# Two halves of a head weighed in a row, y split at its gating, and a second place for transposed weights

## The chip, the core and the metric

The kernel runs on one core of one Trainium2 chip. A core has five engines that run their own instruction streams: TensorE (PE, matrix products; its weight loads are shown as PEld), VectorE (DVE), ScalarE (ACT), GpSimd (POOL) and SyncE (SP), which here only issues transfers. TensorE writes into PSUM, eight banks of 128 partitions; the other data stand in SBUF. The metric is the time of one execution on the device in microseconds; lower is better.

## The reference

The program is two decoder layers over 1024 positions of width 1024, and a last RMS norm. Layer 0 is a gated linear recurrence (RG-LRU), layer 1 is attention with a forget gate (FoX). The change touches layer 1:

```python
u = h @ w_in                      # q, k, v, gate: 16 heads of 64
cum = jnp.cumsum(jax.nn.log_sigmoid(f_logit), axis=1)
logits = q @ k.T * scale + (cum_q - cum_k)
p = jax.nn.softmax(jnp.where(causal, logits, NEG_INF))
o = p @ v                         # "weighing"
y = o * jax.nn.silu(gate)         # "gating"
x = x + y @ w_out
```

## The kernel before

**Numbers in two parts.** Layer 1 keeps float32 accuracy with float16 products: every operand is a high part (the value rounded to float16) and a low part (what is left). A product of two such operands is three matmuls: high by high, low by high, high by low. In the weighing, two of the three share one matmul: V's high and low columns of a head (64 + 64) stand side by side as one 128-wide stationary operand against the high weights ("high", 128 wide), and the low weights go against V's high columns alone ("low", 64 wide). These low matmuls alternate between the left and the right 64 columns of the array, so that two run at a time, and land in the upper or lower half of the same PSUM bank `O`. The two halves of the bank are added when it is read (ScalarE copies one, VectorE adds the other; `yo`).

**Tiling of a head.** Rows (queries) are cut into two halves of 512, `c` = 0 and 1, and these into four blocks of 128. `maxima(hd, c)` does four steps, one for each block `i`: the logits `S` (TensorE, against 128 to 1024 keys), mask and minimum (VectorE, L1086), the exponential (ScalarE), normalised high part `pp` (ScalarE) and low part (VectorE, L1099), and a transposing DMA on SP's queue into `pT` (L1101). `weigh(hd, c)` (L1107) multiplies the transposed weights with V: 4 key blocks for half 0, 8 for half 1, some cut short by causality (512, 384, 256, 128 columns; for half 1 five of 512, then 384, 256, 128). `gated` (L1137) multiplies a pair of heads with its gate `sg`, after the pair's odd head.

**What is woven in.** TensorE is kept busy by other work between these steps: `fill` (the projections for the next pair's q, k and gate, `play`; from head 12 on the partial output projections `partial`, then the last ones in `turned`), and `vals` (V of the next group of four heads, `values_beside`, 16 steps over four heads, a step is 12 matmuls of 256 columns). A fill step is six matmuls of 512 columns.

**What sets the order.** `run` (L1155) plays a string: a digit takes the next step of that generator (0 the weighing, 1 the row blocks), "." a fill step and a piece of a load for T and U (`side`), "v" a value step, "w" a step of the value weights. Each step's TensorE instructions are tied behind the TensorE instruction that was written last (`tc.issue_after`), so the string is TensorE's order. A head has two phases: first `weigh(hd, 0)` beside `maxima(hd, 1)`, then `weigh(hd, 1)` beside `maxima(hd + 1, 0)`. The strings ORDER, TURN, OPEN, START and LAST (L29 to L33) serve plain heads, heads 3 and 7, heads 4 and 8, head 0, and heads 12 to 14; head 15 has its own. What is not tied is placed by a planner, which takes instructions in program order as they become ready and free slots allow, and puts in the semaphores. Each engine then runs its stream in order.

**Places.** A pool tag is a number of slots; a new tile waits until the last reader of the slot's old tile is done. `pT0` and `pT1` (transposed weights of half 0 and 1) have one slot each, `O`, `S` and `g` in PSUM two each. `hT` has two tags of 16 slots of 2 KB: `hh` holds the input of layer 1 (`h16`), `hl` holds 12 gated results `y` in float32 (`kept_y`, pairs 0 to 5), and later x for the first half (`xh`) and results (`res`).

**y.** For pairs 0 to 5 the gated y is kept in float32 (L1145) and split into high and low in heads 12 and 13, beside the last gate projection (`split_loaded`, `beside`): one ScalarE and one VectorE instruction on 128 x 512 for each of 12. Pairs 6 and 7 are split when they are gated (`split_y`).

**Output weights.** `split_out` (L1200) loads `wo` on SP's queue into the three `wf` slots and splits it. `partial` (L1224) fetches x on GpSimd's queue into its `home` and adds the product over pairs 0 to 5.

Of the kernel before, what the change touches and what calls it, by code (L numbers as in the profile page):

```python
# [43 lines left out]
def trunk(ctx: ExitStack, tc: tile.TileContext, xt, w0, wg, wo0, pc, gn, gf, w1, wv, wf, bf, wo1, out):  # L44
# [163 lines left out]
    with nullcontext(ExitStack()) as l0:  # L208
# [8 lines left out]
        def pair():  # L217
            return tuple(hpool.tile([P, HALF], F32R, tag=t, name=t) for t in ("hh", "hl"))
# [48 lines left out]
        raw = [[pair() for k in range(KT)] for h in range(2)]  # L267
# [446 lines left out]
    with ExitStack() as l1:  # L714
# [172 lines left out]
        kept_y = [[hpool.tile([P, HALF], F32, tag="hl", name="y") for pair in range(6)] for c in range(2)]  # L887
# [176 lines left out]
        def maxima(hd, c):  # L1064
# [6 lines left out]
            turned_ = pT[c] = at.tile([P, 4 * c + 4, 2, HALF], FP16, tag=f"pT{c}", name="pT", bufs=1)  # L1071
# [35 lines left out]
        def weigh(hd, c, sub=slice(0, HALF)):  # L1107

            pair, s = hd // 2, hd % 2
            V, turned_ = Vs[pair], pT[c]  # L1110
# [8 lines left out]
            def weighed(to, v, j, t, **kw):  # L1119
                q = max(begin, j * P)  # L1120
                matmul(to[:, q - begin :], v, turned_[:, j, t, q - c * HALF : end - c * HALF], **kw)

            for j in range(nj):
                weighed(O, V[j][:, 2 * s : 2 * s + 2].rearrange("p a d -> p (a d)"), j, 0, start=j == 0, stop=False)
                if j % 2 and j < nj - 1:
                    yield
            for j in range(nj):
                side = (j ^ (j >> 1) if j >= nj - 4 else j) % 2
                weighed(O[side * HD :][:HD], V[j][:, 3 * s], j, 1, start=False, stop=j >= nj - 2)

            r0, r1 = s * HD, (1 - s) * HD
            to, one = yo[r0 : r0 + HD], unit_v[:, hd // 4 : hd // 4 + 1]
            nc.scalar.activation(to, O[r1 : r1 + HD], AF.Copy, scale=one[r1 : r1 + HD])
            nc.vector.scalar_tensor_tensor(to, O[r0 : r0 + HD], one[r0 : r0 + HD], to, ALU.mult, ALU.add)
            yield

        def gated(hd, c, sub=slice(0, HALF)):  # L1137

            if hd % 2 == 0:
                return  # L1140
            pair = hd // 2
            yo = to = yos[pair, c][:, sub]
            if pair < 6:
                to = kept_y[c][pair][:, sub]
            nc.vector.tensor_tensor(  # L1145
                to, yo, sgs[pair][:, c * HALF + sub.start : c * HALF + sub.stop], ALU.mult
            )
            if hd == 15:
                split_y(c, pair, yo, sub)
# [31 lines left out]
        def high_y(c):  # L1181
            for pair in range(6):
                pair_of_y(c, pair)
            yield from ()

        def split_loaded(c):
            for pair in range(6):
                y = kept_y[c][pair]
                split_16(y, *y1[c][pair])
                if pair % 2:  # L1190
                    yield

        def beside(steps, first, more):

            for i, _ in enumerate(steps):
                if i >= first:
                    next(more, None)
                yield
# [70 lines left out]
        def turned(c, q):  # L1269
# [4 lines left out]
            if c == 0:  # L1274
                res = [[hpool.tile([P, HALF], F32, tag="hl", name="res") for h in range(2)] for b in range(2)]
# [100 lines left out]
        for hd in range(HEADS):  # L1376
            pair = hd // 2
            if hd % 2 == 0:
                if hd < 12:
                    fill = play(next(fills))  # L1380
                elif hd == 12:
                    todo = [(db, c) for c in range(2) for db in range(2)]
                    todo += [(db, c) for db in range(2, KT) for c in range(2)]
                    splits = [split_loaded(c) for c in range(2)]
# [20 lines left out]
            run(first, weigh(hd, 0), maxima(hd, 1), fill=fill, side=side, vals=vals, wvals=wvals)  # L1405
# [6 lines left out]
            gated(hd, 0)  # L1412
# [5 lines left out]
            run(second, weigh(hd, 1), maxima(hd + 1, 0), fill=fill, side=side, vals=vals, wvals=wvals)  # L1418
# [3 lines left out]
            drain(side)  # L1422
            gated(hd, 1)
# [7 lines left out]
        run("0..0..0...0..", weigh(15, 1, quarters[0]), fill=fill)  # L1431
        gated(15, 1, quarters[0])
        run("0..0..0..0...0..", weigh(15, 1, quarters[1]), fill=fill)
# [76 lines left out]
```

## Time and profile before

| what | value |
| --- | --- |
| three timed runs | 1020.7, 1019.57, 1020.6 us (median 1020.6) |
| the profiled execution | 1016.93 us |
| its span, first to last instruction | 1015.2 us |
| PE, DVE, ACT, POOL busy | 98%, 78%, 66%, 11% of the span |
| granted TensorE clock | 0.999 |

The profile is of one execution, whose own time differs from the median of the timed runs by 3.7 us. The weighings of the 16 heads start between 527.2 and 994.7 us; layer 0 lies before them, the end of the output projection and the last norm behind. A matmul's shown length includes its way through the array: the next starts before it has ended, so that the distance from start to start is what it costs.

### The profile page before, as it was taken

What the parts mean: (1) busy time and instruction counts of PE and PEld (TensorE: products, weight loads), DVE (VectorE), ACT (ScalarE), POOL (GpSimd) and SP (SyncE); (2) the same over time, 40 slices, a digit from 0 to 9 for tenths busy, and PEclk for the clock granted to TensorE, in tenths of its full rate; (3) what the DMA queues carried; (4) which work ended last, traced back from release to release, by engine and by line L of the source; (5) the groups of instructions that cost most, each with busy time, mean ns of one, the idle gap of its engine ahead of it and who ended that gap; (6) DMA issues with size and microseconds to landing.
All of it is one profiled execution on the core that took longest, in us unless ns stands there. A gap on an engine that the chain in (4) does not pass through costs nothing. (4 is left out here: it accounts for less than half of the span.)

```text
span 1015.2 us, 15117 instructions
## 1 busy us (share of the span) xinstructions
PE 995.4 (98%) x5100; PEld 655.3 (65%) x5100; DVE 788.4 (78%) x1500; ACT 669.1 (66%) x1219; POOL 110.4 (11%) x104
## 2 busy tenths in 40 slices
PE   9999999999999999999999999999999999999997
PEld 6787778888888888776545555555555555444454
DVE  7689585586567557898687988988898878995875
ACT  8469855657657567576684667776667666873655
POOL 1310221222122122000200000000010000001200
PEclk9999999999999999999999999999999999999999
DMA  7211443243334333244366687977688677777954
GB/s 256 62 51 48 126 140 97 91 133 103 124 106 131 96 107 113 70 148 137 85 157 124 122 151 147 193 152 150 130 202 136 138 160 150 154 180 185 231 101 167
DMA packets 219629, 135.88 MB, mean 134 GB/s; under 512 B 162080, under 2 KB 186464, under 8 KB 219552
## 3 DMA queue, kind: packets, MB, share of 16 engines
q1 hardware_dynamic: 216912, 126.27, 51.5%
q0 software_dynamic: 2640, 8.65, 3.1%
q8 instruction: 40, 0.66, 0.3%
q14 instruction: 37, 0.30, 0.1%
HBM read 75.16 MB, written 9.37 MB: 83 GB/s over the span
## 5 line engine op out<-in xcount | busy, mean ns | idle before, releaser
L72 PE MATMUL gps<-h,w 128*128 128x512 f16 x1152 | 268.0, 379 | 0.0
L72 PEld LDWEIGHTS <-w 128*128 128x128 f16 x1440 | 139.9, 98 | 156.3 <-issue 6.8
L60 ACT ACTIVATE p<-p,m 128x128 f32<-128x128 f32 (+7 forms) x128 | 98.9, 772 | 84.1 <-DVE m L1086 75.4
L114 POOL TENSOR_TENSOR wl<-wf,wh 128x512 fp32r<-128x512 f32 x46 | 82.0, 1791 | 315.9 <-ACT wh L60 258.5
L1086 DVE CUSTOM_DVE_ANT_0 p<-S,mask,vsq 128x128 f32<-128x128 f32 (+7 forms) x128 | 103.6, 810 | 14.6 <-PE S L72 14.2
L1099 DVE SCALAR_TENSOR_TENSOR pp<-p,sums,pp 128x128 f16<-128x128 f32 (+7 forms) x128 | 103.4, 812 | 12.2 <-ACT pp L60 11.7
L60 ACT ACTIVATE pp<-p,sums 128x128 f16<-128x128 f32 (+7 forms) x128 | 97.9, 768 | 20.1 <-ACT p L60 14.4
L60 ACT ACTIVATE wsf<-wsf 128x512 f32<-128x512 f32 (+1 forms) x81 | 50.5, 625 | 60.5 <-DMA wsf<-in_w 33.0
L72 PEld LDWEIGHTS <-h 128*128 128x128 f16 x768 | 74.8, 98 | 21.0 <-ACT h L60 1.3
L72 PE MATMUL S<-T,U 128*128 128x512 f16 (+4 forms) x384 | 83.4, 327 | 0.1
L72 PE MATMUL ops<-yh,wh 128*128 128x512 f32 x192 | 77.2, 402 | 1.6 <-ACT yh L60 0.9
L72 PE MATMUL ups<-hh,wh 128*128 128x512 f32 x192 | 76.3, 398 | 1.0 <-ACT hh L60 0.8
L72 PE MATMUL ups<-hl,wh 128*128 128x512 f32 x192 | 76.2, 397 | 0.2 <-DVE hl L275 0.2
L72 PE MATMUL ops<-yh,wl 128*128 128x512 f32 x192 | 75.7, 394 | 0.8 <-DVE wl L114 0.8
L72 PE MATMUL ups<-hh,wl 128*128 128x512 f32 x192 | 75.6, 394 | 0.8 <-POOL wl L114 0.8
L72 PE MATMUL gps<-hh,wh 128*128 128x512 f32 x192 | 75.8, 395 | 0.0
L72 PE MATMUL gps<-hh,wl 128*128 128x512 f32 x192 | 75.5, 393 | 0.1
L72 PE MATMUL gps<-hl,wh 128*128 128x512 f32 x192 | 75.4, 393 | 0.0
L72 PE MATMUL ops<-yl,wh 128*128 128x512 f32 x192 | 74.5, 394 | 0.0
L413 DVE TENSOR_TENSOR x<-x,ops 128x512 f32<-128x512 f32 x80 | 53.7, 679 | 24.8 <-PE ops L72 24.4
L72 PE MATMUL ops<-y,w 128*128 128x512 f16 x288 | 67.5, 379 | 3.5 <-DVE sg L1055 2.2
L72 PE MATMUL vps<-wv,h 128*128 128x256 f16 x576 | 70.4, 273 | 0.0
(253 smaller groups left out, 1764.8 us busy)
## 6 DMA issues: line engine op xcount, KB each, us to landing
wf<-in_w SPq DMA_DIRECT2D x106, 256.0 KB
wsf<-in_w SPq DMA_DIRECT2D x48, 256.0 KB
wf<-in_wo SPq DMA_DIRECT2D x64, 128.0 KB
x<-in_xt SPq DMA_DIRECT2D x16, 256.0 KB
wsf<-in_wv SPq DMA_DIRECT2D x16, 256.0 KB
wsf<-in_wo SPq DMA_DIRECT2D x16, 256.0 KB
x1d<-x SPq DMA_DIRECT2D x16, 256.0 KB
T<-qkh SPq DMA_DIRECT2D x64, 64.0 KB
```

What stands on the lines that cost most here:

```text
L60: act[0] = op(*args, **kw)
L72: pe[0] = nc.tensor.matmul(*args, **kw)
L114: return eng.tensor_tensor(lo, src, f32(hi), ALU.subtract)
L413: nc.vector.tensor_tensor(x, x, pt, ALU.add)
L1086: nc.vector.tensor_tensor_reduce(p, S[:, :n], mask[:, SEQ - n :], unit_s[:, pair : pair + 1], -NEG, ALU.add, ALU.min, accum_out=m)
L1099: nc.vector.scalar_tensor_tensor(both[:, :, 1], p, r, both[:, :, 0], ALU.mult, ALU.subtract)
```

## The change

Four things are edited.

- **Weighing.** Phase one of a head has no weighing any more (the strings lose their "0", a fill step takes its place). Phase two weighs both halves at its end: high of half 0, low of half 0, low of half 1, high of half 1 (`weigh_both`, six steps). Head 15 keeps one half at a time (`weigh_one`). Since the order within half 1 is turned round, each side of the bank notes whether it has been started. TURN loses one "v".
- **A second place for half 0's transposed weights.** Odd heads put them into a new tag `hx` in `hT`, even ones into `pT0` as before. `hx` takes the room of four slots of `hl`, which shrinks from 16 to 12; in layer 0 it holds four low parts of x.
- **y.** For pairs 0 to 5 gating now multiplies with the gate and the scale of y in one VectorE instruction, a ScalarE copy makes the high part and a GpSimd subtraction the low part, into float16 tiles in `hl`. Gating of both halves comes after phase two. `high_y`, `split_loaded` and `beside` go, and what they did beside head 12's and 13's work.
- **Output projection.** The weights for the first two column blocks are loaded on GpSimd's queue at head 12, into the slots that the value weights had (`load_out`). x for the first half and its results go to `hh`.

```diff
-ORDER = "1.v1..1.v1..00", "1.v1..1.v1..0000"
-TURN = "w1v.v1w.w.1w..1w..0000"
-OPEN = "1..1..1..1vv.00", "1..1..1v.1v.0000"
-START = "w1..1.w1..1.00", "1v.1.v.1v.1v.0000"
-LAST = "1..1..1..1..0.0", "1..1.1..1..0..0.0.0"
+ORDER = "1.v1..1.v1...", "1.v1.1.v1..000000"
+TURN = "w1v.1w.w.1w..1w..000000"
+OPEN = "1..1..1..1vv..", "1..1v.1v.1..000000"
+START = "w1..1.w1..1..", "1v.1.v.1v.1v.000000"
+LAST = "1..1..1..1...", "1..1.1..1..0..00.0.00"
...
-            return tuple(hpool.tile([P, HALF], F32R, tag=t, name=t) for t in ("hh", "hl"))
+            return tuple(hpool.tile([P, HALF], F32R, tag=t, name=t, bufs=b) for t, b in (("hh", 16), ("hl", 12)))
...
-        raw = [[pair() for k in range(KT)] for h in range(2)]
+        raw = [[pair() for k in range(KT - 4 * h)] for h in range(2)]
+        low = hpool.tile([P, 4, HALF], F32R, tag="hx", name="hx", bufs=1)
+        raw[1] += [(hpool.tile([P, HALF], F32R, tag="hh", name="hh"), low[:, k]) for k in range(4)]
...
-        kept_y = [[hpool.tile([P, HALF], F32, tag="hl", name="y") for pair in range(6)] for c in range(2)]
+        for c, pair in itertools.product(range(2), range(6)):
+            y = hpool.tile([P, 2, HALF], FP16, tag="hl", name="y16", bufs=12)
+            y1[c][pair] = y[:, 0], y[:, 1]
...
-            turned_ = pT[c] = at.tile([P, 4 * c + 4, 2, HALF], FP16, tag=f"pT{c}", name="pT", bufs=1)
+            if s and c == 0:
+                turned_ = hpool.tile([P, 4, 2, HALF], FP16, tag="hx", name="pT", bufs=1)
+            else:
+                turned_ = at.tile([P, 4 * c + 4, 2, HALF], FP16, tag=f"pT{c}", name="pT", bufs=1)
+            pT[hd, c] = turned_
...
+            begun = [False, False]
+
+            def weighed(to, v, j, t, sides, **kw):
                 q = max(begin, j * P)
+                new = not all(begun[i] for i in sides)
+                for i in sides:
+                    begun[i] = True
+                matmul(to[:, q - begin :], v, turned_[:, j, t, q - c * HALF : end - c * HALF], start=new, **kw)
+
+            def high(last):
+                for j in range(nj):
+                    v = V[j][:, 2 * s : 2 * s + 2].rearrange("p a d -> p (a d)")
+                    weighed(O, v, j, 0, (0, 1), stop=last and j == nj - 1)
+                    if j % 2 and j < nj - 1:
+                        yield
+
+            def low(last):
+                for j in range(nj):
+                    side = (j ^ (j >> 1) if j >= nj - 4 else j) % 2
+                    weighed(O[side * HD :][:HD], V[j][:, 3 * s], j, 1, (side,), stop=last and j >= nj - 2)
...
+        def weigh_one(*args):
+            high, low, out = weigh(*args)
+            yield from high(False)
+            low(True)
+            out()
+            yield
+
+        def weigh_both(hd):
+            high, low, out = weigh(hd, 0)
+            yield from high(False)
+            low(True)
+            out()
+            high, low, out = weigh(hd, 1)
+            low(False)
+            yield
+            yield from high(True)
+            out()
             yield
...
-            yo = to = yos[pair, c][:, sub]
+            yo = yos[pair, c][:, sub]
+            g_ = sgs[pair][:, c * HALF + sub.start : c * HALF + sub.stop]
             if pair < 6:
-                to = kept_y[c][pair][:, sub]
...
+                yh, yl = y1[c][pair]
+                nc.vector.scalar_tensor_tensor(yo, yo, scale_y, g_, ALU.mult, ALU.mult)
+                with tc.issue_after(seen[0].ins):
+                    to_hi(yh, yo, nc.scalar)
+                nc.gpsimd.tensor_tensor(yl, yo, yh, ALU.subtract)
+            else:
+                nc.vector.tensor_tensor(yo, yo, g_, ALU.mult)
...
+        def load_out(db):
+            for k, n in ((0, 4), (4, 2)):
+                raw_o[db, k] = at.tile([P, n, P], F32, tag="wv", name="wof", bufs=4)
+                nc.gpsimd.dma_start(raw_o[db, k], wo1[db, :, k : k + n])
...
-                    wo[db] += cast16(*load16([(wo1[db, :, k : k + n], slice(0, P))], (n, P), None), scale_o)
+                    wt = raw_o[db, k] if db < 2 else load16([(wo1[db, :, k : k + n], slice(0, P))], (n, P), None)[0]
+                    wo[db] += cast16(wt, None, scale_o)
...
-                x = hpool.tile([P, HALF], F32, tag="hl", name="xh")
+                x = hpool.tile([P, HALF], F32, tag="hh", name="xh")
...
-                res = [[hpool.tile([P, HALF], F32, tag="hl", name="res") for h in range(2)] for b in range(2)]
+                res = [[hpool.tile([P, HALF], F32, tag="hh", name="res") for h in range(2)] for b in range(2)]
...
-                        high_y(0),
                         first_out(),
-                        beside(play(last_g[1]), 1, splits[0]),
-                        high_y(1),
-                        beside(partial(todo), 3, splits[1]),
+                        play(last_g[1]),
+                        partial(todo),
...
-            run(first, weigh(hd, 0), maxima(hd, 1), fill=fill, side=side, vals=vals, wvals=wvals)
+            weighing = weigh_one(15, 0) if hd == HEADS - 1 else iter(())
+            run(first, weighing, maxima(hd, 1), fill=fill, side=side, vals=vals, wvals=wvals)
...
-            gated(hd, 0)
...
-            run(second, weigh(hd, 1), maxima(hd + 1, 0), fill=fill, side=side, vals=vals, wvals=wvals)
+            run(second, weigh_both(hd), maxima(hd + 1, 0), fill=fill, side=side, vals=vals, wvals=wvals)
...
+            gated(hd, 0)
             gated(hd, 1)
```

More of the change, by code (lines that the diff above doesn't have):

```diff
@@ L1127, in weigh @@
[L1127 to L1134, printed above, removed]
+                new = not all(begun[i] for i in sides)
@@ new lines, in out @@
+            def out():
+                r0, r1 = s * HD, (1 - s) * HD
+                to, one = yo[r0 : r0 + HD], unit_v[:, hd // 4 : hd // 4 + 1]
+                nc.scalar.activation(to, O[r1 : r1 + HD], AF.Copy, scale=one[r1 : r1 + HD])
+                nc.vector.scalar_tensor_tensor(to, O[r0 : r0 + HD], one[r0 : r0 + HD], to, ALU.mult, ALU.add)
+            return high, low, out
+        def weigh_one(*args):
[4 more added lines that the diff above has]
+            yield
@@ L1179, in split_y @@
             split_16(y, yh, yl)
[L1181 to L1198, printed above, removed]
+        raw_o = {}
+        def load_out(db):
+            for k, n in ((0, 4), (4, 2)):
+                raw_o[db, k] = at.tile([P, n, P], F32, tag="wv", name="wof", bufs=4)
+                nc.gpsimd.dma_start(raw_o[db, k], wo1[db, :, k : k + n])
         def split_out(db):
@@ L1430, in trunk @@
         gated(15, 0)
-        run("0..0..0...0..", weigh(15, 1, quarters[0]), fill=fill)
+        run("0..0..0...0..", weigh_one(15, 1, quarters[0]), fill=fill)
         gated(15, 1, quarters[0])
-        run("0..0..0..0...0..", weigh(15, 1, quarters[1]), fill=fill)
+        run("0..0..0..0...0..", weigh_one(15, 1, quarters[1]), fill=fill)
         gated(15, 1, quarters[1])
```

14 lines of the change are left out of this document (3 added, 11 removed).

## The prediction

> **What bounds the kernel now.** I read the page first, then the stages by windows, then TensorE's waits, then the timeline around the weighing.
>
> ```profile
> span 1015.2 us, 15117 instructions
> PE 995.4 (98%) x5100; PEld 655.3 (65%) x5100; DVE 788.4 (78%) x1500; ACT 669.1 (66%) x1219; POOL 110.4 (11%) x104
> 527.00:871.80 344.80, 344.56 (x2053) 189.90 (x2054) 291.21 (x693) 230.66 (x448) 4.81 (x9) 1.00 0.75 152
> 871.80:897.00 25.20, 24.35 (x128) 11.39 (x127) 24.10 (x53) 22.76 (x43) 1.07 (x2) 1.00 0.74 146
> 897.00:934.00 37.00, 35.67 (x180) 16.58 (x179) 28.56 (x66) 18.59 (x35) 5.91 (x12) 1.00 0.86 198
> 934.00:963.60 29.60, 28.19 (x142) 12.71 (x141) 22.01 (x51) 18.50 (x33) 5.92 (x14) 1.00 0.93 208
> ```
>
> The columns of a window are its length, then PE, PEld, DVE, ACT and POOL busy, the granted clock, and the DMA share. From 527 to 872 us (heads 0 to 11) PE is busy for 344.56 of 344.80 us at clock 1.00. VectorE has 54 us free there, ScalarE 114. So in the heads only PE's own work counts, and an edit on ScalarE, VectorE or GpSimd is free as long as it does not make PE wait. From 872 to 897 the picture differs: VectorE is full (24.10 of 25.20).
>
> The waits that are left are few:
>
> ```profile
> 527.24 1.11 PE L72 MATMUL O<-pT,v 128*128 128x512 f16 x8 [1.26 <-DMA pT<-pp]
> 893.30 2.75 PE L72 MATMUL ops<-y,w 128*128 128x512 f16 x12 [0.85 <-DVE sg L1055]
> 899.33 1.02 PE L72 MATMUL ops<-y,w 128*128 128x512 f16 x4 [1.33 <-DVE sg L1055]
> 940.12 1.46 PE L72 MATMUL ops<-y,w 128*128 128x512 f16 x6 [0.66 <-DVE xh L1239]
> 945.78 1.46 PE L72 MATMUL ops<-y,w 128*128 128x512 f16 x6 [0.46 <-DVE sums L1096]
> 960.42 1.46 PE L72 MATMUL ops<-y,w 128*128 128x512 f16 x6 [0.18 <-DVE xh L1239]
> 982.25 0.66 PE L72 MATMUL turn<-ident,xh 128*128 128x128 f32 x4 [1.16 <-DVE res L1305]
> ```
>
> Now the cost that is hidden inside "busy". These are two weighings of one head, low weights included, and what stands around them:
>
> ```profile
> 700.82 2.75 PE L72 MATMUL gps<-h,w 128*128 128x512 f16 x12
> 703.41 1.10 PE L72 MATMUL O<-pT,v 128*128 128x512 f16 x8
> 704.44 0.29 PE L72 MATMUL S<-T,U 128*128 128x128 f16 x2
> ...
> 713.34 2.75 PE L72 MATMUL gps<-h,w 128*128 128x512 f16 x12
> 715.93 2.40 PE L72 MATMUL O<-pT,v 128*128 128x512 f16 x16
> 718.25 0.72 PE L72 MATMUL S<-T,U 128*128 128x320 f16 x4
> ```
>
> Starts are what counts, since the shown lengths overlap. Twelve matmuls of 512 columns take from 713.34 to 715.93, 0.216 us each. Half 0 streams 512 + 384 + 256 + 128 = 1280 columns at full width, 0.54 us, and the same 1280 for the low weights, which are 64 wide and run two at a time, 0.27 us: 0.81. It takes 703.41 to 704.44, 1.03. Half 1 has 3328 columns twice: 1.40 + 0.70 = 2.10, and takes 715.93 to 718.25, 2.32. Both are 0.22 us over, though one is 2.6 times as long as the other. The excess therefore belongs to the change of width (128 to 64 and back), not to the columns.
>
> **The change, part by part.**
>
> *Two halves in a row.* The sequence high 0, low 0, (other work), high 1, low 1 becomes high 0, low 0, low 1, high 1, and high 1 runs on into 128-wide work. One of two excursions into 64-wide work goes. Heads 0 to 14 do it, head 15 keeps its old form: 15 x 0.22 = **3.3 us** less. No column is added. The unknown is whether low 0 to low 1, into another bank, is free. Inside one group the low matmuls already alternate between the two sides of the array, and the excess of 0.22 did not grow from 4 of them to 8, so I take it as free; if it cost as much as half an excursion the saving would be 1.6. The Trainium skill (TensorEngine Tiling (Array Packing), Key Properties) says that changing the tiling mode, "not just tile", drains TensorE. By that rule low to low costs nothing and the term is 3.3; by the bound above it is 1.6.
>
> *The price of it: two output banks at once.* Low 1 needs its bank O while half 0's is still being read. The pool has two. In most heads the other bank was last used by a value projection (vps), finished before 4 us of other PE work, and its readers are four short ones (rows below: 2 x 0.36 + 2 x 0.34 = 1.4 us). TURN (heads 3 and 7) loses a "v": 15 of 16 value steps are then done when the weighing starts, vps is half built and holds a bank until the drain behind the weighing. There low 1 waits for half 0's readers, 0.68 + 0.74 = 1.42 us. No order ties the 12 left-over vps matmuls (1.31 us, first row) behind it, so they can fill that hole, at the cost of one more excursion of 0.22.
>
> ```profile
> 705.86 1.47 PE L72 MATMUL vps<-wv,h 128*128 128x256 f16 x12
> 707.17 0.38 PE L72 MATMUL S<-T,U 128*128 128x256 f16 x2
> L60 ACT ACTIVATE yo<-O,wsq x33: 467/681/685, 528.4 to 995.1; 64x512 f32<-64x512 f32 x31, 64x256 f32<-64x256 f32 x2
> L1134 DVE SCALAR_TENSOR_TENSOR yo<-O,wsq,yo x33: 490/743/758, 529.5 to 995.9; 64x512 f32<-64x512 f32 x31, 64x256 f32<-64x256 f32 x2
> L60 ACT ACTIVATE v<-vps,rv x64: 345/359/428, 477.2 to 854.0; 128x128 f16<-128x128 f32 x64
> L795 DVE SCALAR_TENSOR_TENSOR v<-vps,rv,v x64: 314/343/352, 477.9 to 855.3; 128x128 f16<-128x128 f32 x64
> ```
>
> Between filled (2 x 0.22 = 0.4) and not filled (2 x 1.6 = 3.2) I take **0.8 us** more, nearer to filled, because the planner issues what is ready.
>
> *Half 0 a phase later, with a second place for pT.* Weighing 0 of head 0 stood waiting 1.26 us for its transposes (527.24). It now comes behind the next head's four row blocks, some 12 us later. The pitch of a matmul is 0.163 us under its shown 0.379 (715.93 above: 0.216), and idle is counted from the shown end, so the hole is **1.4 us**, all of it gone. The next S there writes a bank whose reader ended long before, so I see nothing late behind it; kept end: 0. In the other heads half 0's transposes gain slack, half 1's keep the whole second phase as now. Without the second place the next head's transposes would overwrite weights that are not yet weighed; it costs memory, no instruction. The wait for pT1 (one place) sits on SP's queue as before, and behind it the loads of T and U, with the same phase to spare. Fill steps per head stay the same or grow by one.
>
> *y split at the gating.* These go out of the stretch 880 to 895, where they stand in front of the evictions that PE waits for:
>
> ```profile
> L1145 DVE TENSOR_TENSOR y<-yo,sg x12: 681/684/693, 567.5 to 861.4; 128x512 f32<-128x512 f32 x12
> L60 ACT ACTIVATE y<-y,outs x12: 707/711/723, 880.0 to 891.9; 128x512 f16<-128x512 f32 x12
> L1175 DVE SCALAR_TENSOR_TENSOR y<-y,outs,y x12: 721/733/734, 881.6 to 894.8; 128x512 f16<-128x512 f32 x12
> L60 ACT CAST qkh<-gps 128x512 f16<-128x512 f32 x3 | 1.7, 576 | 1.1 <-DVE gps L783 1.1
> L114 POOL TENSOR_TENSOR wl<-wf,wh x46: 1284/1298/3311, 8.9 to 395.9; 128x512 fp32r<-128x512 f32 x46
> ```
>
> 8.8 us of VectorE (12 x 0.733) and 8.5 us of ScalarE (12 x 0.711) leave 15 us in which VectorE had no idle time. The two waits for sg there, 0.85 + 1.33 + 2 x 0.16 = **2.5 us**, should go whole; bounds 0 and 2.5. What comes in their place lies in heads 1 to 11: the multiply of 0.68 becomes one with a scale (0.73), 12 ScalarE copies of some 0.58 (by the cast) = 7 us into 114 free, 12 GpSimd subtractions of 1.3 us on an engine busy 4.8 of 345 us. Nobody reads y before 893. If that cover were gone they would cost 0.6 + 7 + 15.6 us.
>
> *Weights and places of the output projection.* Four loads of wo move from SP's queue to GpSimd's, and their place is free once the last value weights are used (853.1, first row below). x for half 0 can now be fetched only when h is free; last_g[0] frees it four fill steps (5.2 us) ahead of the first partial, which then takes three more. The waits at 940 to 960 (0.66 + 0.46 + 0.18 + 3 x 0.16 = 1.8) hang on ScalarE standing for weights:
>
> ```profile
> L72 PE MATMUL vps<-wv,h x576: 272/273/273, 528.4 to 853.1; 128*128 128x256 f16 x192
> 936.43 0.72 ACT L60 ACTIVATE w<-wf,outs 128x512 f16<-128x512 f32 x1 [6.41 <-DMA wf<-in_wo]
> 937.18 0.75 DVE L738 SCALAR_TENSOR_TENSOR w<-wf,outs,w 128x512 f16<-128x512 f32 x1 [4.75 <-ACT w L60]
> ```
>
> SP has four loads fewer ahead of these, but DMA is at 0.86 to 0.93 and PE arrives earlier. Bounds: 1.8 less to 1.5 more (PE's earlier arrival); I take **0.4** less. The tail from 964 keeps its work, with x and results in other slots; 0, bounds 1 either way (its one wait, 1.16).
>
> Sum: 3.3 - 0.8 + 1.4 + 2.5 + 0.4 = **6.8 us** less. The profiled execution took 1016.93 us for a span of 1015.2; it should come to 1010.1. The three timed runs have a median of 1020.6, 3.7 above that execution, and I forecast on their scale: **1013.8 us**.
>
> **The rivals.**
>
> *The waits move.* VectorE is free earlier, PE reaches the partial products earlier, but the weights' DMA is not earlier, and what was saved at 893, 899 and 527 is waited for again. Then 3.3 - 0.8 = 2.5 remain: 1018.1. For it: the 6.41 above and DMA at 0.93. Against: the two waits for sg name VectorE, not a DMA.
>
> *The second bank is late in every head with value steps*, not only in TURN's two. At 0.5 us in each of 12 heads, 6.0 of the 6.8 go: 1019.8. For it: START puts only one fill step (1.3 us) and half 0 (0.8) between the last v and low 1. Against: readers of 1.4 us, and VectorE 84% busy (291 of 345).
>
> *The slower side: GpSimd's subtractions hold VectorE.* While one GpSimd subtraction ran, a VectorE instruction on 12 elements took 1.25 us, and another, shortly after, on 12 elements took 0.16:
>
> ```profile
> 55.00 1.88 POOL L114 TENSOR_TENSOR wl<-wf,wh 128x512 fp32r<-128x512 f32 x1 [6.70 <-ACT wh L60]
> 55.65 1.25 DVE L238 TENSOR_TENSOR sp_d<-sp_e 128x12 f32<-128x12 f32 x1
> 60.40 0.16 DVE L241 SCALAR_TENSOR_TENSOR sp_q<-sp_q,sp_d 128x12 f32<-128x12 f32 x1
> ```
>
> So 12 subtractions can hold VectorE 12 x 1.3 = 15.6 us in the heads. If all of it reached PE: 1020.6 - 6.8 + 15.6 = 1029.4; it turns the sign once more than 6.8 / 12 = 0.57 us of each gets through. Against: 54 us are free on VectorE, and PE has two S banks and two g banks in hand. The Trainium skill (SBUF — State Buffer, Who interferes with whom) states it as a lock: a VectorE instruction with two SBUF inputs and a GpSimd one that reads SBUF exclude each other, and the loser waits whole. The row at 55.65 agrees.
>
> *It does nothing*: the planner sets the halves apart, or the excess stays: 1020.6.
>
> **How the numbers follow.** My forecast has 0.70, the moving waits 0.13, the late bank 0.08, GpSimd's hold 0.05, nothing 0.04. About 0.2% (2.0 us) is what a measurement of this kernel tells from no change. Faster takes the forecast and most of the first rival, 0.80; same the rest of that, the late bank and nothing, 0.13; slower the hold and the worse part of the late bank, 0.07. All terms at their good ends give 3.3 - 0.4 + 1.4 + 2.5 + 1.8 + 1 = 9.6: 1011.0, and the runs spread by 1 us: lower end 1010. The upper end, 1019, takes in the moving waits and leaves the other three out.
>
> **What would show it.** One change to 64 columns and back per head, with 3.1 us from start to start for 2.9 of columns; no wait at the first weighing; no VectorE row for y (L1175) between 880 and 895 but for pairs 6 and 7; the waits for sg gone. I am wrong if PE waits inside the weighing, if a wait for VectorE appears after an odd head, or if the waits from 934 on grow by more than 2 us.

## The result and the profile after

Six runs of the changed kernel have a median of 1013.85 us, six of the kernel before beside them 1019.45: the ratio is 0.9946, 95% interval 0.9933 to 0.9958, 5.6 us less. A second series gave 1015.7 against 1018.98, ratio 0.9967 (0.9953 to 0.9982), 3.3 us less. The change is faster, by 3 to 6 us.

The profiled executions took 1016.93 and 1015.43 us, only 1.5 apart. That of before lies 2.5 under its median, that of after 1.6 above its own, so the profiles show where time comes and goes, not all of the medians' difference. The page and the stages by windows after:

```profile
span 1013.6 us, 15158 instructions
PE 992.8 (98%) x5100; PEld 655.4 (65%) x5100; DVE 784.3 (77%) x1488; ACT 667.4 (66%) x1219; POOL 127.3 (13%) x120
527.00:871.80 344.80, 342.08 (x2043) 189.54 (x2041) 292.64 (x692) 236.30 (x460) 20.01 (x23) 1.00 0.76 152
871.80:897.00 25.20, 24.96 (x131) 11.74 (x129) 20.89 (x51) 17.86 (x36) 2.17 (x4) 1.00 0.85 165
897.00:934.00 37.00, 37.00 (x189) 17.50 (x187) 26.96 (x61) 18.61 (x35) 5.96 (x12) 1.00 0.80 188
934.00:963.60 29.60, 27.55 (x141) 12.90 (x140) 21.80 (x52) 17.13 (x32) 6.78 (x14) 1.00 1.04 198
```

From 872 to 897 VectorE fell from 24.10 to 20.89 and PE gained 0.6; the next window has no idle time left. But in the first window 2.7 us of PE's time are now idle where 0.24 were, and from 934 on PE is less busy than before, with the DMA share at 1.04 (it was 0.93). The timeline of PE after, weighing and waits:

```profile
712.75 3.32 PE L72 MATMUL O<-pT,v 128*128 128x512 f16 x24
715.90 0.71 PE L72 MATMUL S<-T,U 128*128 128x320 f16 x4
...
644.80 0.38 PE L72 MATMUL vps<-wv,h 128*128 128x256 f16 x2 [0.68 <-DVE wv L809]
757.55 0.60 PE L72 MATMUL vps<-wv,h 128*128 128x256 f16 x4 [0.66 <-DVE wv L809]
864.42 2.55 PE L72 MATMUL gps<-h,w 128*128 128x512 f16 x11 [0.40 <-DVE w L740]
868.63 3.84 PE L72 MATMUL gps<-h,w 128*128 128x512 f16 x17 [0.58 <-DVE w L740]
941.10 1.46 PE L72 MATMUL ops<-y,w 128*128 128x512 f16 x6 [0.74 <-DVE xh L1268]
954.02 1.43 PE L72 MATMUL O<-pT,v 128*64 128x512 f16 x10 [0.49 <-DMA pT<-pp]
958.00 1.46 PE L72 MATMUL ops<-y,w 128*128 128x512 f16 x6 [0.82 <-DVE xh L1268]
965.96 0.54 PE L72 MATMUL O<-pT,v 128*128 128x512 f16 x2 [0.88 <-DMA pT<-pp]
```

Both halves in a row take 3.15 us from start to start (712.75 to 715.90); apart they took 1.03 + 2.32 = 3.35. The waits for pT at the first weighing and for sg are gone. New are waits for value weights (heads 4 and 8), for gate weights (864, 868), and for transposes at the end; those for x have grown (0.74 and 0.82, before 0.66 and 0.18).

To compare traces step by step I use landmarks: the start of a head's first logits of half 1 (the beginning of its phase one). There both kernels have done the same weighings and, in plain heads, the same other work. A kernel's own difference at the start of head 0 (between -1.3 and +1.0 us, which no edit explains) is taken off. In us; negative is earlier than before:

| kernel | head 3 | 5 | 9 | 12 | 13 | 14 | 15 | last `turn` |
| --- | --- | --- | --- | --- | --- | --- | --- | --- |
| after | -1.9 | -1.3 | -0.8 | -1.4 | +0.7 | -2.1 | -2.0 | -0.5 |
| after, second profile | -1.9 | -1.7 | -1.4 | -2.0 | 0.0 | -2.8 | -2.6 | -1.2 |
| e1, v kept | -1.9 | +2.6 | +8.6 | +8.8 | +10.3 | +7.6 | +9.0 | +9.0 |
| e6, v kept, subtraction moved | -1.9 | -0.2 | +0.5 | -0.2 | +1.4 | -1.4 | -1.9 | +0.1 |
| e2, halves apart | -1.4 | -0.6 | -0.4 | -0.1 | +1.4 | -1.1 | +1.7 | +1.8 |
| e3, weighing alone | -1.9 | -2.1 | -2.8 | -3.5 | -3.7 | -2.1 | -2.4 | -2.0 |
| e4, y alone | -0.1 | +0.2 | +0.2 | +0.2 | +0.7 | -1.8 | +0.6 | +0.6 |
| e7, wo on SP's queue | -1.9 | -1.9 | -0.6 | -1.2 | -1.5 | +4.2 | +4.0 | +4.3 |
| e8, x not loaded | -1.9 | -1.8 | -1.1 | -1.1 | +0.3 | -2.4 | -3.0 | -3.0 |
| e9, subtraction moved | -1.9 | -2.1 | -2.8 | -3.5 | -1.9 | -4.6 | -6.0 | -4.3 |
| e10, and wo held | -1.9 | -1.5 | -1.3 | -2.0 | -2.2 | -5.0 | -6.6 | -4.6 |
| e11, e9 and x early | -1.9 | -2.1 | -2.8 | -3.3 | -1.7 | -4.4 | -2.8 | -2.8 |
| e12, e10 and gains held | -1.9 | -1.8 | -1.1 | -1.8 | -2.0 | -4.8 | -5.5 | -5.5 |

Of the 1.6 us between the two spans, 1.0 lie ahead of head 0. From there to the last `turn` the changed kernel gained 0.5 us in one profile and 1.2 in the other. The parts gained far more; most was given back.

### The profile page after: what moved, and what is told of

Same layout as the page of the kernel before. It is cut to its first block, busy times and chain, and to the rows that moved or that the text cites. A ratio compares the mean times of both kernels' runs of the same rounds, so it can differ in the third digit from the quotient of the medians.

```text
span 1013.6 us, 15158 instructions
## 1 busy us (share of the span) xinstructions
PE 992.8 (98%) x5100; PEld 655.4 (65%) x5100; DVE 784.3 (77%) x1488; ACT 667.4 (66%) x1219; POOL 127.3 (13%) x120
## 5 line engine op out<-in xcount | busy, mean ns | idle before, releaser
L1107 DVE SCALAR_TENSOR_TENSOR pp<-p,sums,pp 128x128 f16<-128x128 f32 (+7 forms) x128 | 104.2, 818 | 11.2 <-ACT pp L60 10.3
L60 ACT CAST wh<-wf 128x512 fp32r<-128x512 f32 x72 | 43.6, 610 | 34.7 <-PE ops L72 20.3
L72 PE MATMUL O<-pT,v 128*128 128x512 f16 (+7 forms) x396 | 57.0, 324 | 1.6 <-DMA pT<-pp 1.6
```

The costliest lines, as they stand in the source:

```text
L60: act[0] = op(*args, **kw)
L72: pe[0] = nc.tensor.matmul(*args, **kw)
L1107: nc.vector.scalar_tensor_tensor(both[:, :, 1], p, r, both[:, :, 0], ALU.mult, ALU.subtract)
```

## The experiments

Their medians stand against runs of the kernel before on the same chip. The runs of one kernel spread by 2 to 9 us, so places are read from the landmarks and the verdict from the interval.

**e1, the v that TURN lost put back.**

```diff
-TURN = "w1v.1w.w.1w..1w..000000"
+TURN = "w1v.v1w.w.1w..1w..000000"
```

> The changed kernel with one edit: TURN (heads 3 and 7) gets its second "v" back, so the last value projection of a group ends before the weighing. Theory A (the missing v is what makes PE wait for value weights at 644.8 and 757.6 us, because the old weights' places come free only behind the weighing): both waits (idle 0.68 and 0.66, with the pipeline's 0.16 each 0.84 and 0.82) go, and two excursions into 64 columns (2 x 0.22) with them: about 2.1 us less than the changed kernel, near 1011.8. Theory B (those casts are late for another cause, ScalarE's or the DMA's): the waits stay, 1013.9 within 0.7. Theory C (my forecast's bank): the projection's readers now hold the bank that low 1 needs, PE waits inside the weighing of heads 3 and 7 by 0.5 us or more each: 1013 or more.

1025.97 against 1017.59 us, ratio 1.0083 (1.0065 to 1.0101): slower than the kernel before. Theory C's open end (1013 or more) takes the number in, but not for its reason: PE does not wait inside the weighing of heads 3 and 7. The landmarks lose 4.4 us at head 4 and 6.4 at head 8. GpSimd's queue and PE there:

```profile
632.26 0.54 POOL L815 DMA_DIRECT2D wvf<-in_wv  x1 [5.87 <-DVE wv L809]
638.83 3.02 POOL L1185 TENSOR_TENSOR y<-yo,y 128x512 f16<-128x512 f32 x2 [6.02 <-ACT y L60]
641.80 0.56 POOL L815 DMA_DIRECT2D wvf<-in_wv  x1
...
646.97 0.56 PE L72 MATMUL vps<-wv,h 128*128 128x256 f16 x2 [2.85 <-ACT wv L60]
```

GpSimd's stream is in order and also issues the loads of the value weights. Two subtractions of y stand in it ahead of a load; they wait for ScalarE, and the load goes out only when both, 3.02 us, are done. The next load, cast and load hang on the same single place (`wvf`), and PE waits. The waits have a second price. Behind them the granted clock, the last column but two, was 0.51:

```profile
647.00:650.50 3.50, 3.27 (x11) 1.50 (x11) 2.50 (x6) 3.50 (x6) 0.54 (x1) 0.51 0.89 176
763.00:770.00 7.00, 5.23 (x15) 2.15 (x15) 4.81 (x11) 3.72 (x6) 0.00 (x0) 0.51 0.90 166
```

e6 below has the same order on PE. Against it e1 falls back by another 1.3 us in the first of these stretches and by 2.5 in the second, together 3.8 of the 8.95 us that lie between the two at head 12. In the changed kernel, whose clock stays at 1.00 there, it is one subtraction ahead of the load:

```profile
636.81 1.22 POOL L1185 TENSOR_TENSOR y<-yo,y 128x512 f16<-128x512 f32 x1 [5.61 <-ACT y L60]
637.97 0.56 POOL L815 DMA_DIRECT2D wvf<-in_wv  x1
645.05 0.54 POOL L815 DMA_DIRECT2D wvf<-in_wv  x1 [6.53 <-DVE wv L809]
```

**e2, the same phase, but low 1 behind high 1.**

```diff
-            low(False)
-            yield
-            yield from high(True)
+            yield from high(False)
+            low(True)
```

> The changed kernel with the order in phase two back to high 0, low 0, high 1, low 1: same place in the string, same work, but two excursions into 64 columns a head. Theory A (the saving is the change of width, 0.22 us for each excursion, whatever stands around it): 15 x 0.22 = 3.3 us more than the changed kernel, near 1017.2. Theory B (the gain of the weighing comes from its later place, transposes in time, and the width costs nothing that other waits don't hide): within 0.8 of 1013.9. Half of it (1015.5) would say that low 0 to low 1 costs half an excursion.

1017.96 against 1017.59, 1.0005 (0.9992 to 1.0018). From head 2 to 3 and from 9 to 11 its landmarks are flat to 0.01 us where those with the halves in a row gain 0.22 to 0.23 per head. That is the price of one change to 64 columns and back, measured by taking it away. So theory A holds for the heads. The wait at the first weighing goes here too (-1.43 at head 2).

**e3 and e4, each half of the change alone.** e3 keeps the old y and output weights; e4 keeps the old weighing.

```diff
 e3
-            nc.vector.scalar_tensor_tensor(yo, yo, scale_y, g_, ALU.mult, ALU.mult)
+            nc.vector.tensor_tensor(to, yo, g_, ALU.mult)
 e4
-            run(second, weigh_both(hd), maxima(hd + 1, 0), ...
+            run(second, weigh(hd, 1), maxima(hd + 1, 0), ...
```

> The weighing part alone: strings, both halves in a row, second place for pT; y is kept in float32 and split in heads 12 and 13 as before, output weights on SP's queue; x for half 0 and half of the results stand in other places. Theory A (terms by the trace): 15 x 0.22 = 3.3 and the first wait, 1.2 to 1.4, less some 2.1 for TURN: 2.5 us under the kernel before, near 1017.0, and the two waits for sg between 880 and 900 (2.5 us) still there. Theory B (the split of y gave nothing, the weighing all): 1013.9. Theory C (the weighing gave nothing): 1019.5.

> The y part alone on the kernel before: y split at the gating with GpSimd's subtraction, first output weights on GpSimd's queue, x for half 0 and results in hh; strings and weighing as before. Theory A: the two waits for sg go (2.5 us), against that the gate weights at head 12 may come late as they do in the changed kernel (idle 0.22 + 0.40 + 0.58 + 0.16, up to 1.7 us): 0.8 to 2.5 under the kernel before, 1017.0 to 1018.7. Theory B (GpSimd's subtractions hold VectorE and PE pays): 1019.5 or more, with waits for VectorE behind odd heads. Theory C (the weighing gave nothing, y all): 1013.9.

e3: 1016.04 against 1017.59, 0.9979 (0.9966 to 0.9993). e4: 1017.73, 1.0002 (0.9991 to 1.0014). e3 reaches head 12 at -3.5, with the same TURN and no subtraction on GpSimd: no wait for value weights. It then waits for sg, and for 2.27 us in a weighing at 921.45:

```profile
895.95 1.46 PE L72 MATMUL ops<-y,w 128*128 128x512 f16 x6 [1.69 <-DVE sg L1057]
```

e4 gains exactly 2.5 us from head 13 to 14, where the waits for sg had been, as theory A said, but its time is that of the kernel before: it loses 2.4 from 14 to 15:

```profile
936.32 1.02 PE L72 MATMUL S<-T,U 128*128 128x512 f16 x4 [1.68 <-DVE m L1088]
944.98 1.46 PE L72 MATMUL ops<-y,w 128*128 128x512 f16 x6 [1.31 <-DVE xh L1234]
960.14 1.46 PE L72 MATMUL ops<-y,w 128*128 128x512 f16 x6 [0.87 <-DVE xh L1234]
```

**e6, e1 with four subtractions moved** (beside it e5, the changed kernel again).

```diff
-                nc.gpsimd.tensor_tensor(yl, yo, yh, ALU.subtract)
+                lower = nc.vector if hd in (3, 7) else nc.gpsimd
+                lower.tensor_tensor(yl, yo, yh, ALU.subtract)
```

> The changed kernel again, unedited, beside its variants on one chip, so that they are read against it and not against another day's runs. Both theories: its ratio to the kernel before as recorded, 0.993 to 0.996.

> TURN gets its "v" back, and in heads 3 and 7 alone y's low part is subtracted on VectorE instead of GpSimd (4 of 12). Restoring the v alone made PE wait 2.85 and 4.06 us for value weights, behind a load that GpSimd issued 2.5 us late. Theory A (GpSimd's queue: the subtractions, which wait for the gating, stand ahead of the chained loads of the value weights): without them the loads go out as soon as the cast frees their place, no wait for value weights at heads 4 and 8, and two excursions less than the changed kernel: 2.1 us under it. Theory B (the value weights are late because the weighing's and y's casts on ScalarE and VectorE push theirs back): the waits stay within 1 us of what they were with the v, 8 to 12 us over the changed kernel.

e6: 1015.83 against 1018.98, 0.9977 (0.9962 to 0.9992), against e1's 1.0083: the queue made most of e1's loss, by its waits and by the halved clock behind them. e5 has 0.9967, just above what was expected, and e6 is no faster than it, as theory A had said it would be: a wait for value weights stays in head 4:

```profile
646.17 0.60 PE L72 MATMUL vps<-wv,h 128*128 128x256 f16 x4 [1.54 <-DVE wv L809]
```

From head 3 to 5 it loses 1.6 us where e9 below gains 0.2. So with the v the chain of loads is too slow by itself, and dropping the v was right.

**e7, the output weights back on SP's queue**, where `split_out` loads them when it needs them.

```diff
-                    wt = raw_o[db, k] if db < 2 else load16([...], (n, P), None)[0]
+                    wt = load16([...], (n, P), None)[0]
```

> The changed kernel with the first output weights loaded on SP's queue like the others (no loads of wo on GpSimd's queue at 845 to 850 us). PE waits there for gate weights at 863 to 877 (idle 0.22 + 0.40 + 0.58 + 0.16). Theory A (the early loads of wo crowd the DMA queues and the gate weights land late): these waits go, 1.0 to 1.7 us less by head 13. Theory B (the gate weights' loads are issued late on SP, behind T, U and transposes): the waits stay within 0.3, and the time within 0.8 of the changed kernel, or more if the wo loads push others back.

1021.16 against 1018.98, 1.0016 (1.0005 to 1.0028). The waits for gate weights at 863 to 877 go, but others come:

```profile
898.70 0.61 PE L72 MATMUL ops<-y,w 128*128 128x512 f16 x1 [3.47 <-ACT w L60]
926.54 1.43 PE L72 MATMUL O<-pT,v 128*64 128x512 f16 x10 [1.65 <-DMA pT<-pp]
949.21 1.45 PE L72 MATMUL ops<-y,w 128*128 128x512 f16 x6 [1.80 <-DVE sums L1104]
```

So the early loads cause the gate weights' wait, and without them the kernel is 5.5 us slower than the changed one beside it. This loss, too, is not waiting alone. The order on PE is that of the changed kernel; behind the wait of 3.47 us the granted clock was 0.50, and there e7 falls back by another 2.4 us:

```profile
897.50:904.30 6.80, 5.42 (x13) 1.90 (x14) 3.66 (x7) 4.71 (x8) 0.00 (x0) 0.50 0.63 154
```

**e8, less traffic at the end.** Five of the sixteen loads of x (half 1, blocks 3 to 7) are replaced by zeros, so this output lacks x there.

> The changed kernel without the loads of x for five of the eight column blocks of the second half (zeros in their place; 5 x 256 KB less on GpSimd's queue between 907 and 967 us), so that the output lacks the residual there. Theory A (from 934 us the DMA queues are full, and what PE saved earlier is given back there as waits for x and for pT): the waits for pT and xh from 934 to 966 (0.74 + 0.49 + 0.82 + 0.88) shrink to under 1 us, and it ends 2 us or more under the changed kernel. Theory B (the waits come from the order on the engines, not from the amount of DMA): within 0.8 of the changed kernel.

1012.3 against 1018.98, 0.9938 (0.9926 to 0.995). From head 14 to the last `turn` it gains 0.6 us where the changed kernel loses 1.6. The waits for pT at 954 and 966 are gone; one for x stays (1.65 us at 943.33). The DMA share is down from the changed kernel's 1.04:

```profile
934.00:964.00 30.00, 28.35 (x147) 13.33 (x145) 24.41 (x59) 18.57 (x34) 6.74 (x14) 1.00 0.85 198
```

**e9, the changed kernel with the four subtractions moved as in e6.** PE's order is that of the changed kernel, instruction by instruction.

> The changed kernel, but the four subtractions of the y of heads 3 and 7 (TURN's heads) run on VectorE instead of GpSimd; the order on TensorE is the same to the instruction. In the changed kernel TensorE waits 0.66 to 0.68 us by the rows, 0.84 by the landmarks, for value weights in head 4 and again in head 8. Theory A: GpSimd's queue makes them late, because the subtraction stands in it ahead of the fourth load of value weights and waits 5.6 us for ScalarE; then both waits go, the start of head 5 stays 2.7 us ahead of before (it fell back to 1.85) and the kernel takes 1.7 us less than the changed one. Theory B: the chain of loads and casts through the one raw place is late by itself, as the run with the v kept and these subtractions on VectorE showed waits of 1.5 us; then waits of 0.5 us or more stay at both places and the time is within 0.5 us of the changed kernel.

Theory A. Both waits for value weights are gone, and head 12 is at -3.46, as in e3. GpSimd's queue, and ScalarE's cast at the end of its load:

```profile
637.69 0.54 POOL L815 DMA_DIRECT2D wvf<-in_wv  x1 [5.48 <-DVE sums L1105]
644.50 0.54 POOL L815 DMA_DIRECT2D wvf<-in_wv  x1 [6.28 <-DVE wv L809]
...
641.67 0.72 ACT L60 ACTIVATE wv<-wvf,wsq 128x512 f16<-128x512 f32 x1 [0.51 <-DMA wvf<-in_wv]
```

The time was 1015.05 against 1018.23, 0.9969 (0.9951 to 0.9987), with runs from 1012.3 to 1018.6: the 2 us that the landmarks show by head 12 are too few to tell from the changed kernel by that.

**e10, e9 with the loads of wo held** until head 11's y is split.

```diff
+                nc.gpsimd.tensor_copy(raw_o[db, k][:, 0, :1], y1[db][5][1][:, :1])
                 nc.gpsimd.dma_start(raw_o[db, k], wo1[db, :, k : k + n])
```

> As the run before it, and the four loads of wo on GpSimd's queue are held (by a copy of one column) until the subtractions of head 11's two halves are done: some 860 and 866 us in place of 845 to 851. Theory A: these loads, 0.77 MB, share the DMA engines with the transposes on SP's queue at 847 to 852 (two took 4.76 us where one took 3.03 before), SP comes late to the gate weights, and PE waits 2.1 us for them between 863 and 877; with the loads held the two transposes and the gate weights are about 1.5 us earlier and 1.5 to 2 us are gained over the run before it. Theory B: the loads only collide elsewhere, with the transposes of 866 to 874 where the DMA engines are full; then the waits between 863 and 877 go but 1 us or more comes back as waits for wo or transposes by 905, and the time is the same within 1 us.

1012.09 against 1018.23, 0.9944 (0.993 to 0.9959). SP's queue of the changed kernel, then of e10, and the window 846 to 852 of both (same columns as the prediction's windows):

```profile
847.22 4.76 SPq L1109 DMA_TRANSPOSE pT<-pp  x2
852.03 0.58 SPq L69 DMA_DIRECT2D T<-qkh  x1
858.32 1.26 SPq L1109 DMA_TRANSPOSE pT<-pp  x1
859.63 1.06 SPq L69 DMA_DIRECT2D wf<-in_w  x2
846.00:852.00 6.00, 6.00 (x36) 3.36 (x35) 4.99 (x19) 4.36 (x12) 1.58 (x3) 1.00 1.09 255
```

```profile
846.41 2.88 SPq L1109 DMA_TRANSPOSE pT<-pp  x1
849.35 0.64 SPq L69 DMA_DIRECT2D T<-qkh  x1
856.92 0.59 SPq L69 DMA_DIRECT2D wf<-in_w  x1
857.61 1.25 SPq L1109 DMA_TRANSPOSE pT<-pp  x1
846.00:852.00 6.00, 6.00 (x36) 3.33 (x34) 4.75 (x19) 4.62 (x13) 0.00 (x0) 1.00 0.91 182
```

Theory A in the time: the waits for gate weights are gone, and from head 12 to 13 e10 gains 0.2 us, what a plain head gains, where e9 loses 1.6 and the changed kernel 2.1. Its mechanism holds in part. Counted from the start of head 12's logits of half 1, the first load of gate weights leaves SP after 1.3 us, in e9 after 3.3. Of these 2.0 us, 1.3 are order: in the changed kernel and in e9 a transpose (858.32) stands ahead of the gate weights in SP's queue, in e10, e7 and e3 it stands behind the first of them (857.61). T's load and a transpose have changed places too, so the 4.76 us above are two transposes (3.48 and 1.19), against one. About 0.7 us are slower traffic: in e10 SP is that much earlier once the same transposes are done. The first transpose of these rows kept SP busy for 3.25 to 4.93 us in the nine kernels that load wo beside it, for 2.88 to 3.21 in the five that do not. The Trainium skill (DMA: Bandwidth & Descriptors, Issuing engines are not separate DMA queues) states that transfers interleave on the same 16 engines whoever starts them. The trace agrees, by these few tenths. The window's DMA share does not tell the two apart: the kernel before, without these loads, has 1.16 there. Why the planner chose another order is not shown, and no run changes the loads alone. e4 comes nearest: it loads wo early, has the gate weights ahead of the transpose, and loses 0.4 us from head 12 to 13.

On ScalarE and VectorE the order changed in heads 4 to 11 as well, and e10 is 1.5 us behind e9 by head 12, with waits of 0.34 and 0.35 us inside two weighings.

**e11, e9 with the loads of x one partial product earlier.**

```diff
-                if before[-2] is not None and (c, db) in homes:
+                if before[-3] is not None and (c, db) in homes:
```

> As the first of these three, and the loads of x behind the partial products are each held until the third last partial product instead of the second last: 2.6 us earlier, with the same bytes. Theory A: the stretch 934 to 964 is bound by what the DMA engines can carry (share 1.04), so the same bytes earlier change little: the waits for xh (0.74 and 0.82 us) shrink and those for transposes grow, and the time is within 1 us of the first of the three. Theory B: only the lead is too short, 5.5 us (two partial products) for loads that take 6.0 us to land; with 8 us of lead both waits go and 1.5 to 2 us are gained.

1013.54 against 1018.23, 0.9959 (0.9946 to 0.9972): the same as e9 within the intervals. Theory A had the waits for xh shrink; they grew (in e9 there is one, of 0.59 us), and from head 14 on e11 gives back 1.6 us where e9 gives back 0.3:

```profile
939.39 1.45 PE L72 MATMUL ops<-y,w 128*128 128x512 f16 x6 [1.01 <-DVE xh L1269]
953.09 1.43 PE L72 MATMUL O<-pT,v 128*64 128x512 f16 x10 [1.27 <-DMA pT<-pp]
957.46 1.46 PE L72 MATMUL ops<-y,w 128*128 128x512 f16 x6 [1.21 <-DVE xh L1269]
```

More lead without fewer bytes did not help, which is theory A's forecast for the time.

**e12, e10 with the last gains held** until they no longer compete with the last loads of x.

```diff
+                nc.gpsimd.tensor_copy(g_[:, :1], homes[0, 7][:, :1])
                 nc.gpsimd.dma_start(g_, gf[:, cs].to_broadcast([P, HALF]))
```

> As the run with the held output weights, and the two loads of the last gains (grow, 0.26 MB each, for the tail only) are held until the partial product 7 of half 0 is evicted, some 962 us in place of 952; the same bytes. Theory A: what is left between 950 and 965 is the DMA engines' capacity; with 0.5 MB out of the full stretch the transposes that PE waits for at 961.95 (1.38 us by the row) land earlier and 1 to 1.5 us are gained over the held output weights (1012.09 median there), while the gains land at 967, ahead of their first use at 973. Theory B: that wait hangs on SP's queue or on VectorE and not on the load of the DMA engines; then the wait stays and the time is the same within 1 us, or the gains come late and a wait for res in the tail grows by 1 us or more.

1010.68 us against 1019.63, ratio 0.9909 (0.9892 to 0.9925): theory A, and faster than both kernels: its interval lies under the changed kernel's 0.9933 to 0.9958. Against e10, by the landmarks, it gains 0.9 us, all of it behind head 14; the two ran on different chips, so their medians say less. The wait for pT at 961.95 is gone (one of 0.51 us comes at 973.17), the share in 934 to 964 falls from 0.99 to 0.94. In head 8 a wait of 0.63 us for value weights is back, though no subtraction stands ahead of their load there: the chain through `wvf` has next to no slack. The wait for res, late in the tail, shrank as well; the changed kernel's row, then e12's:

```profile
980.74 0.44 PE L72 MATMUL turn<-ident,xh 128*128 128x128 f32 x2 [1.24 <-DVE res L1334]
```

```profile
934.00:964.00 30.00, 28.60 (x148) 13.47 (x147) 22.56 (x52) 17.08 (x32) 5.64 (x12) 1.00 0.94 186
976.63 0.55 PE L72 MATMUL turn<-ident,xh 128*128 128x128 f32 x3 [0.49 <-DVE res L1337]
```

## Why the prediction was right or wrong

1013.8 us were forecast and 1013.85 measured, but that is in good part luck. The repeat gained 3.3 us, not 6.8. For a profiled execution the prediction said 1010.1; the two took 1015.43 and 1014.41. By the landmarks the terms that held were offset by losses that the sum did not have.

The signs that it named came: one change of width a head, no wait at the first weighing, no y beside the evictions, no wait for sg. Two of its signs of being wrong came as well: PE waits inside weighings (0.18 us at 685.83, 0.49 at 954.02), and for VectorE's value weights after the odd heads 3 and 7. The waits from 934 on grew by 1.7 us, not by more than 2.

- **The switch of width, 15 x 0.22.** Right in mechanism and in size per head: 0.226 us, and e2 gets none. It counted 15 heads; by head 14's landmark eleven show it: one of heads 0 and 1 (0.22 more than e2 at head 2), the plain ones of 2 to 11, and 12 and 13. That is 11 x 0.226 = 2.5. TURN's two heads do not, because the planner put the left-over vps between the halves, as foreseen (the sum had paid for that in TURN's term), and the next head's first work as well: half 1 starts 7.5 us behind half 0's end (rows below). Low 0 to low 1 in another bank costs nothing that can be seen (3.15 us from start to start for 2.9 of columns). So the rule of the Trainium skill which the prediction cited (TensorEngine Tiling (Array Packing), Key Properties: "not just tile") gave the right term, and the bound of 1.6 did not apply.

```profile
627.86 1.16 PE L72 MATMUL vps<-wv,h 128*128 128x256 f16 x9
635.32 2.41 PE L72 MATMUL O<-pT,v 128*64 128x512 f16 x16
```

- **TURN, 0.8.** The place was right, and the filled hole's 0.4 came as the two excursions; but PE never waited for the second bank, and the rest of the loss has another cause. The step that failed stands in the part on y: "12 GpSimd subtractions ... on an engine busy 4.8 of 345 us" at no cost: how busy an engine is says nothing of what is queued behind a waiting instruction. The prediction looked at what stands in SP's queue, but not at GpSimd's, which issues the value weights' loads. Price by the landmarks: 0.84 in head 4 and 0.81 in head 8, and 0.38 for transposes between heads 5 and 7, where e9 has no such wait: 2.0 us by head 12 (-1.42 against e9's -3.46). The second profile shows 1.5.
- **The first wait, 1.4.** Right: 1.43 by e2's landmark at head 2.
- **sg, 2.5.** Right, whole: 2.50 in e4 from head 13 to 14, and 2.74 after, with 0.23 of the switch.
- **Weights and places, 0.4 less (1.8 less to 1.5 more).** Wrong, in two places. "SP has four loads fewer" is true of the queue, but SP still comes late to the gate weights: with the early loads a transpose stands ahead of them, and the transposes run slower (1.3 and 0.7 us in e9 against e10). Head 12 to 13 loses 2.3 us (+2.07 where e10 gains 0.22). And the end gives back 1.6 from head 14 on. Together 3.9 us against a bad bound of 1.5 (2.5 with the tail's).
- Sum of the terms to the last `turn`: -1.4 - 2.5 - 2.5 + 2.0 + 2.3 + 1.6 = -0.5 us, what the table has. The sum of 6.8 lacked 5.9 us of losses, nearly all at waits that go back to a load or a transpose.
- **The rivals.** "The waits move" came true in part: from 934 on, where DMA is full, not at 893 or 899. "GpSimd's subtractions hold VectorE": no. e9, with eight of the subtractions on GpSimd, reaches head 12 at the same -3.46 as e3, which has none; whatever they held did not reach PE. By VectorE's rows they held little: three low parts of weights (`pp`, 640 wide) that ran beside one took 1.07 to 1.16 us where that shape else takes 0.88, and four products `yo` 0.81 for 0.75, some 1 us in all against the 15.6 that the rival allowed. One took 1.16 us, near the price of 1.3, by the row of the changed kernel (shortest, median and longest in ns; below it one `pp` alone and one beside a subtraction). "The second bank" and "does nothing": no.

```profile
L1185 POOL TENSOR_TENSOR y<-yo,y x12: 1147/1160/1261, 577.0 to 864.2; 128x512 f16<-128x512 f32 x12
664.81 0.88 DVE L1107 SCALAR_TENSOR_TENSOR pp<-p,sums,pp 128x640 f16<-128x640 f32 x1
693.33 1.15 DVE L1107 SCALAR_TENSOR_TENSOR pp<-p,sums,pp 128x640 f16<-128x640 f32 x1
```

Open is where the rest of the medians' difference lies. Only one execution of before has a trace, and it lies 2.5 us under the median. Open too is why the end takes back so differently (0.1 us in e3, 0.3 in e9, 1.6 after, 2.8 in e2); that e8 and e12, the two that lighten it, are the only ones that gain there (0.6 and 0.7) points to the DMA engines, but not to a rule for the others.

## What to carry to other kernels

Moving work to an idle engine is free only if nothing that others wait for is queued behind it: on an engine that also issues transfers, list the loads behind the moved instruction and what it waits for. Moving a load to another queue can change what both queues do around it; before a load is sent early, look at what is in flight in that stretch and at the order of the queue that it left, and hold it until a gap when its first use is far off. A gain ahead of a stretch in which DMA is full can be given back there: here the two kernels that lightened it gained in it, and the others lost 0.1 to 2.8 us. After a long wait of TensorE read the granted clock before the loss is put down to the wait alone.

## What the runs showed of the hardware

- One change of TensorE from 128-wide to 64-wide products and back costs 0.226 us, the same in every plain head; low to low in another bank costs nothing that can be seen.
- Behind long waits of TensorE the granted clock was halved for a while: 3.4 us behind a wait of 2.85 (e1), 6.8 behind one of 3.47 (e7) and with two of 2.07 and 1.99 close together (e1). That cost another 1.3, 2.4 and 2.5 us. From head 0 on, single waits of up to 2.27 us (e3) left it at 1.00. The timed runs bear it out: their mean clocks are 0.992 to 0.996 in e1 and 0.995 to 0.996 in e7, against 0.997 to 1.0 in the kernel before beside them.
- Plain loads of 768 KB on another queue made the transpose beside them slower by a few tenths of a us (3.25 us and more for 2.88 to 3.21), while PE was busy in the whole window in both cases: what they cost appeared 12 us later, at another load in the transposes' queue.
- Two profiles of one kernel agree to 0.02 us at the landmarks up to head 4 and at heads 6 to 8; they differ by 0.4 us at head 5 and by 0.5 to 0.7 from head 9 on. In those stretches that is the size below which one profile shows nothing.
